# Merge of a hybrid decoder layer: the samples' columns of the attention's values are prepared in one step, apart from the prompt's

## The chip, the cores and the metric

The kernel runs on one core of one Trainium2 chip. The metric is the device time of one execution in microseconds (us), the median of the runs shown; lower is better.

## What is computed

One step of a decoder layer with two parallel branches: stick-breaking attention and a state space layer. It handles a prompt of 1024 tokens and 8 samples of one token each, whose columns are kept side by side (1024 + 8 = 1032 columns, channels on the partitions). The part that matters here is the end, where the branches meet; the reference, cut to it:

```python
def _finish(x, gate, o_att, g_att, y_ssm, m_att, m_ssm, w_att_out, w_out, ln_g, ln_b):
    y_att = (o_att.reshape(bsz, s, D_ATT) * jax.nn.silu(g_att)) @ w_att_out
    merged = jax.nn.sigmoid(m_att) * y_att + jax.nn.sigmoid(m_ssm) * y_ssm
    return _layer_norm(DEEPNORM_ALPHA * x + gate * (merged @ w_out), ln_g, ln_b)
```

`o_att` are the attention's values, `silu(g_att)` their gate, `y_ssm` the output of the state space layer's own last product (`y @ w_ssm_out`). `gate` comes from a small product of the conditioning vector with `w_cond`.

## The kernel before

All large products are made in float32 accuracy out of three products of halves: an operand is split into `hi`, its value rounded by a cast on ScalarE (ACT), and `lo`, the rest, by a subtraction on VectorE (DVE). `gemm` (L124 to L144) makes one slab of 128 output channels: 8 input blocks, 3 thirds of 344 columns and 3 pairs of halves, 72 matmuls in all, into three PSUM tiles `pj`; its weights `whi` and `wlo` are split while the slab before runs.

The order of TensorE (PE) is that in which the program is written. `Stream` holds the queue of slabs; `weave` (L211 to L222) deals a list of other steps evenly between the matmuls: in front of each step it runs a share of what is left of the slabs in the queue. Its argument `until` is the amount of slab work at which it stops. The order of the other engines and of the DMA queues is set by a scheduler that plans with estimated times; it too is fixed when the program is built. An instruction that waits holds up all that stands behind it on its engine.

The merge, at the end of the program (from L1614 on), runs four groups of eight slabs and then the output product:

- `glu` (L1224), the gated unit of the state space layer.
- `ssm_out` (L1251), its output product. Slab f is evacuated on DVE with three products (L1261, tile `m`, which came from `d_mm`) and written to `d_pa` (L1262).
- `att_out` (L1291), the attention's output product over `act_a`, the eight split blocks of the attention's values; it adds what lies in `d_pa`.
- `finish` (L1359), the output product and the normalization.

Three kinds of small work are dealt into `ssm_out`. First the rest of `LateValues` (L845): the samples' attention reads the last pages of its value cache here, by gathers into `l_t`, products (L884) and sums (L885) on DVE, a last addition (L888), and then writes the samples' values to `d_o` in memory (L889). They are woven in until 5 slabs are left (L1635). Then, by L1636, two lists of eight steps each, dealt alternately over what is left:

- `gate_steps` (L1321): a gate part is four matmuls (L343, tile `gp`) on a block of `w_cond` that was loaded (L327) and split (L334 on ACT, L335 on DVE). The halves `wchi` and `wclo` have one buffer each, so the split for the next part starts behind the matmuls of this one.
- `open_a` (L1268): step f prepares one block of the attention's values. Three loads of 512 KB, the values in two halves and their gate (`x` at L1198, `olo` at L1278, `sga` at L1279), an addition (L1280) and a product (L1281) on DVE make the prompt's 1024 columns. For the samples' 8 columns, a row block `orow` of 8 × 128 is loaded from `d_o` (L1283), transposed on PE (L1285, tile `otp`) and multiplied by its gate `sgs` on DVE (L1286). Then all 1032 columns are split in one go: a cast on ACT (L234) and a subtraction on DVE (L235).

Buffers couple these. The tag `wc` has four: the gathered `l_t`, the blocks of `w_cond`, `olo`, `sga` and later blocks of `w_out` take them in turn. The tag `x` has two. The PSUM tiles `gp` and `otp` share two buffers of one tag.

Of the kernel before, what the change touches and what calls it, by code (L numbers as in the profile page):

```python
# [9 lines left out]
F32 = mybir.dt.float32  # L10
F32R = mybir.dt.float32r
I32 = mybir.dt.int32
AF = mybir.ActivationFunctionType
ALU = mybir.AluOpType
# [3 lines left out]
NP, NS, NT = 1024, 8, 1032  # L18
NC3, CW = 3, 344
KT = 8  # L20
# [8 lines left out]
MM = 146.0  # L29
# [4 lines left out]
HURRY = 400  # L34
# [6 lines left out]
NLATE = 26  # L41
GS = "v"
LATE = 5.0
AHEAD = 2
DRAIN = 1.6
TWO_PI = 6.283185307179586
# [35 lines left out]
def blk(i, w=128):  # L82
    return slice(w * i, w * i + w)
# [141 lines left out]
def weaved(a, b):  # L225

    n = [((i + 0.5) / len(x), j, s) for j, x in enumerate((a, b)) for i, s in enumerate(x)]
    return [s for _, _, s in sorted(n, key=lambda e: e[:2])]


def split_act(k, pool, src):
    hi = pool.tile([128, NT], F32R, tag="hi", bufs=KT, name="ahi")
    lo = pool.tile([128, NT], F32R, tag="lo", bufs=KT, name="alo")
    k.nc.scalar.copy(hi, src)  # L234
    k.nc.vector.tensor_tensor(lo, src, hi.bitcast(F32), ALU.subtract)  # L235
    return hi, lo
# [301 lines left out]
class Attention:  # L538
# [130 lines left out]
    def turn(self, p, h, m, j):  # L669

        k, nc, pool = self.k, self.k.nc, self.pool
        PE, ACT, DVE = nc.tensor, nc.scalar, nc.vector
        w = [self.w[p, h, 2 * m + e][0] for e in range(2)]
        tp = self.ps.tile([128, 4, 128], F32, tag="wt", name="tp")
        if j < m:
            hi, lo = (pool.tile([128, 4, 128], F32R, tag=n, bufs=LAG + 1, name=n) for n in ("wthi", "wtlo"))
        else:
            hi, lo = self.diag
        order = (0, 1) if j < m else (1, 0)
        for a in order:  # L680
            for e in range(2):
                if j < m or (a, e) != (1, 0):
                    PE.transpose(tp[:, 2 * order[a] + e], w[e][:, blk(2 * j + a)], k.ident)  # L683
        with k.tc.high_priority(HURRY):
            s = slice(0 if j < m else 1, 4)
            ACT.copy(hi[:, s], tp[:, s])  # L686
            DVE.tensor_tensor(lo[:, s], tp[:, s], hi[:, s].bitcast(F32), ALU.subtract)  # L687
        return hi, lo
# [39 lines left out]
    def steps(self, pairs):  # L728

        units = [(p, h, ms) for p in pairs for h in range(2) for ms in ((3, 0), (2, 1))]  # L730
        out = {p: [] for p in pairs}
        for u, (p, h, ms) in enumerate(units):
            s = self.score_steps(units[u + 1]) if u + 1 < len(units) else []
            t = [(860, (lambda key=(p, h, m): self.ready_at[key]) if j == ORDER[m][0] else None,
                  lambda t=(p, h, m, j): self.turn_step(t)) for m in ms for j in ORDER[m]]
            if not s:
                t += [(430, None, lambda: self.turn_step(None))] * LAG
            seq = []
            for n in (2, 2, 1, 1):
                seq += s[:n] + t[:1]  # L740
                s, t = s[n:], t[1:]
            out[p] += seq + t
        return self.score_steps(units[0]), out
# [101 lines left out]
class LateValues:  # L845
# [25 lines left out]
    def step(self, n):  # L871

        k, nc = self.k, self.k.nc
        if n < 8 * self.pages:
            self.load(n // 8, n % 8)
        n -= AHEAD
        if n < 0:
# [13 lines left out]
    def steps(self):  # L891
        return [(0, None, lambda n=n: self.step(n)) for n in range(8 * self.pages + AHEAD)]

# [296 lines left out]
class Merge:  # L1190
# [77 lines left out]
    def open_a(self):  # L1268

        k, nc = self.k, self.k.nc  # L1270
        self.a_guard = self.pool("seta", "right")
        pa = self.a_guard.__enter__()
        self.act_a = []

        def one(f):
            t = self.load(k.d_a[f, 0], "x", NP)
            o, s = (self.ld.tile([128, NP], F32, tag="wc", bufs=4, name=n) for n in ("olo", "sga"))
            nc.sync.dma_start(o, k.d_a[f, 1])  # L1278
            nc.sync.dma_start(s, k.d_sa[f])  # L1279
            nc.vector.tensor_tensor(t[:, 0:NP], t[:, 0:NP], o, ALU.add)  # L1280
            nc.vector.tensor_tensor(t[:, 0:NP], t[:, 0:NP], s, ALU.mult)  # L1281
            ob = self.ld.tile([NS, 128], F32, tag="orow", bufs=2, name="orow")
            nc.sync.dma_start(ob, k.d_o[:, blk(f)])  # L1283
            tp = k.psg.tile([128, 512], F32, tag="g", name="otp")
            nc.tensor.transpose(tp[:, 0:NS], ob, k.ident[0:NS, 0:NS])  # L1285
            nc.vector.tensor_tensor(t[:, NP:NT], tp[:, 0:NS], k.sgs[:, f], ALU.mult)  # L1286
            self.act_a.append(split_act(k, pa, t))

        return [(110, None, lambda f=f: one(f)) for f in range(KT)]

    def att_out(self):  # L1291
        k, nc = self.k, self.k.nc
# [160 lines left out]
def stickbreak_s5_kernel(ctx: ExitStack, tc: tile.TileContext, io, out):  # L1453
    nc = tc.nc
    k = Ctx()
# [55 lines left out]
    S = k.stream = Stream(k)  # L1511
# [108 lines left out]
    mg = Merge(k, io, out)  # L1620
# [12 lines left out]
    mg.open_gate()  # L1633
    mg.ssm_out()
    S.weave(late[NLATE:], LATE * KT * 9 * MM)  # L1635
    S.weave(weaved(mg.gate_steps(), mg.open_a()))  # L1636
    mg.s_guard.__exit__(None, None, None)
    mg.att_out()
    mg.open_out()
# [60 lines left out]
def build(nc, arrays):  # L1700
    from concourse import mybir as _mybir
    io = {n: nc.dram_tensor("in_" + n, v.shape, _mybir.dt.from_np(v.dtype), kind="ExternalInput").ap()
          for n, v in arrays.items()}
    out = {n: nc.dram_tensor("out_" + n, s, F32, kind="ExternalOutput").ap() for n, s in _OUTS}
    with tile.TileContext(nc, schedule_with_timeline_sim=True) as tc:
        stickbreak_s5_kernel(tc, io, out)
# [12 lines left out]
```

## Time and profile before

| | |
|---|---|
| median of 3 runs | 1613.56 us (1612.72 to 1615.05) |
| the profiled execution, its own time | 1617.42 us |
| span in its profile, first to last instruction | 1615.7 us |
| PE busy | 1489.5 us, 92% of the span |
| DVE, POOL (GpSimd), ACT busy | 1218.9, 911.0, 736.5 us |
| mean granted clock of PE | 0.969 |
| PE busy in 1300 to 1350, 1350 to 1414, 1414 to 1504 us | 32.75 of 50, 60.05 of 64, 90.00 of 90 us |

A row of a timeline gives start and duration in us, the engine, the line of the kernel, the operation, what it writes and reads by the program's names, the shape, and in brackets how long the engine stood idle ahead of it and what ended that. `SPq` and `ACTq` are the issues of DMAs by those engines. Matmuls overlap: the rows last 0.32 us where one starts every 0.16, so the distance of starts is what counts. A row of the waits gives the total, the number of times and the longest. The chain of waits goes back from the last instruction, at each step to what released it.

### The profile page before, as it was taken

What the parts mean: (1) busy time and instruction counts of PE and PEld (TensorE: products, weight loads), DVE (VectorE), ACT (ScalarE), POOL (GpSimd) and SP (SyncE); (2) the same over time, 40 slices, a digit from 0 to 9 for tenths busy, and PEclk for the clock granted to TensorE, in tenths of its full rate; (3) what the DMA queues carried; (4) which work ended last, traced back from release to release, by engine and by line L of the source; (5) the groups of instructions that cost most, each with busy time, mean ns of one, the idle gap of its engine ahead of it and who ended that gap; (6) DMA issues with size and microseconds to landing.
All of it is one profiled execution on the core that took longest, in us unless ns stands there. A gap on an engine that the chain in (4) does not pass through costs nothing.

```text
span 1615.7 us, 25524 instructions
## 1 busy us (share of the span) xinstructions
PE 1489.5 (92%) x9321; PEld 1410.2 (87%) x9321; DVE 1218.9 (75%) x1717; ACT 736.5 (46%) x1360; POOL 911.0 (56%) x744
## 2 busy tenths in 40 slices
PE   8899999999999999999989978889979786999997
PEld 4789999999999998999888978889779685899885
DVE  5558888888888888743899978787489975744566
ACT  3557777777776776643433333333432212311200
POOL 1738787878777877766566555552176541132164
PEclk9899999999999999999999989999989997999999
DMA  9323433334343434348789887875546677954322
GB/s 356 111 82 89 104 100 97 99 97 113 87 113 93 115 88 111 101 123 288 246 266 287 265 265 249 285 235 132 164 158 222 213 249 261 348 180 140 118 79 91
DMA packets 176731, 275.47 MB, mean 170 GB/s; under 512 B 46395, under 2 KB 119867, under 8 KB 176477
## 3 DMA queue, kind: packets, MB, share of 16 engines
q1 hardware_dynamic: 150555, 180.40, 36.6%
q0 software_dynamic: 23456, 84.95, 16.4%
q10 hardware_dynamic: 2594, 8.49, 2.0%
q8 instruction: 73, 1.20, 0.3%
q14 instruction: 53, 0.43, 0.1%
HBM read 196.77 MB, written 66.24 MB: 163 GB/s over the span
## 4 chain that ended last, share of the span: by engine, by line
PE 49%; DVE 26%; DMA 9%; issue 5%; ACT 3%; POOL 2%; SPq 1%; DVEq 0%; ACTq 0%; POOLq 0%
PE pj L141 32%; PE f L1397 6%; DVE s_sc L828 4%; PE o L700 3%; PE z L654 3%; PE tp L683 3%; DVE ke L665 3%; DVE l_t L884 2%; DMA s_t<-in_cache_k,s_idx 2%; DVE be L666 2%; DVE vs L636 2%; DMA l_t<-in_cache_v,l_idx 2%; DVE l_acc L885 2%; DVE wlo L109 1%; DVE xs L1037 1%
## 5 line engine op out<-in xcount | busy, mean ns | idle before, releaser
L141 PE MATMUL pj<-ahi,whi 128*128 128x344 f32 x2112 | 695.4, 331 | 36.8 <-ACT u L970 17.5
L141 PE MATMUL pj<-alo,whi 128*128 128x344 f32 x2112 | 686.1, 326 | 7.9 <-DVE alo L1220 4.1
L141 PE MATMUL pj<-ahi,wlo 128*128 128x344 f32 x2112 | 581.6, 328 | 6.0 <-POOL wlo L109 6.0
L141 PEld LDWEIGHTS pj<-ahi,whi 128*128 128x128 f32 x2112 | 405.6, 192 | 45.9 <-ACT u L970 18.3
L141 PEld LDWEIGHTS pj<-alo,whi 128*128 128x128 f32 x2112 | 405.6, 192 | 11.9 <-DVE alo L235 4.9
L141 PEld LDWEIGHTS pj<-ahi,wlo 128*128 128x128 f32 x2112 | 382.6, 192 | 8.0 <-POOL wlo L109 6.5
L665 DVE TENSOR_TENSOR_SCAN ke<-ke,eye 128x896 f32<-128x896 f32 (+7 forms) x128 | 217.7, 1701 | 92.4 <-ACT ke L655 92.2
L109 POOL TENSOR_TENSOR wlo<-w,whi 128x1024 fp32r<-128x1024 f32 x53 | 141.6, 2672 | 207.7 <-ACT whi L108 178.8
L108 ACT CAST whi<-w 128x1024 fp32r<-128x1024 f32 x90 | 94.9, 1055 | 137.3 <-PE pj L141 100.1
L655 ACT ACTIVATE ke<-z,nhb 128x448 f32<-128x448 f32 (+2 forms) x192 | 111.8, 582 | 81.1 <-PE z L654 79.2
L666 DVE TENSOR_TENSOR be<-be,ke 128x896 f32<-128x896 f32 (+7 forms) x128 | 128.0, 1000 | 13.0 <-ACT wthi L686 0.5
L828 DVE SCALAR_TENSOR_TENSOR s_sc<-s_t,s_q,s_sc 128x512 f32<-128x512 f32 x126 | 114.0, 905 | 18.0 <-DMA s_t<-in_cache_k,s_idx 12.0
L656 ACT ACTIVATE be<-z,hb 128x448 f32<-128x448 f32 (+2 forms) x192 | 110.6, 576 | 0.0
L807 POOL DMA_INDIRECT s_t<-in_cache_k,s_idx x64 | 70.6, 1103 | 50.8 <-DVE s_sc L828 15.5
L683 PE MATMUL tp<-ident,be 128*128 128x128 f32 x576 | 88.9, 272 | 0.0
L493 POOL TENSOR_TENSOR pt<-tab 128x256 f32<-128x256 f32 x64 | 79.5, 1241 | 3.1
L492 POOL TENSOR_TENSOR pr<-tab 128x256 f32<-128x256 f32 x32 | 25.9, 811 | 89.4 <-DMA tab<-d_tab 78.7
L1520 ACT ACTIVATE gate<-pj 128x344 f32<-128x344 f32 x72 | 32.7, 458 | 95.4 <-PE pj L141 86.5
L109 DVE TENSOR_TENSOR wlo<-w,whi 128x1024 fp32r<-128x1024 f32 x37 | 62.5, 1689 | 15.4 <-ACT whi L108 15.3
L686 ACT CAST wthi<-tp 128x512 fp32r<-128x512 f32 x96 | 56.7, 590 | 32.3 <-PE tp L683 29.9
L654 PE MATMUL z<-kl,qs 128*128 128x448 f32 (+2 forms) x192 | 66.0, 344 | 4.0 <-DMA kl<-kl 4.0
L687 DVE TENSOR_TENSOR wtlo<-tp,wthi 128x512 fp32r<-128x512 f32 x96 | 65.3, 680 | 5.7 <-ACT wthi L686 5.7
(314 smaller groups left out, 2758.5 us busy)
## 6 DMA issues: line engine op xcount, KB each, us to landing
w<-in_w_in SPq DMA_DIRECT2D x38, 512.0 KB
w<-in_w_in POOLq DMA_DIRECT2D x26, 512.0 KB, 5.6
wc<-in_w_cond SPq DMA_DIRECT2D x24, 512.0 KB
d_a<-ox SPq DMA_DIRECT2D x128, 64.0 KB
gst<-d_gg SPq DMA_DIRECT2D x8, 576.0 KB
x<-in_xr SPq DMA_DIRECT2D x9, 512.0 KB
xt<-in_xt SPq DMA_DIRECT2D x8, 516.0 KB
d_sg<-gate SPq DMA_DIRECT2D x8, 516.0 KB
```

What stands on the lines that cost most here:

```text
L108: nc.scalar.copy(whi, w32)
L109: self.eng.tensor_tensor(wlo, w32, whi.bitcast(F32), ALU.subtract)
L141: PE.matmul(ps[c], w[:, blk(t)], x[:, cs(c)], start=(t == 0 and i == 0), stop=(t == KT - 1 and i == 2))
L493: POOL.tensor_tensor(t1, c, d, ALU.mult)
L654: nc.tensor.matmul(z[:, 0:wide], st["q", h][:, blk(i)], x[:, s:s + wide], start=j == 0, stop=j == 1)
L655: nc.scalar.activation(ke[:, s:s + cw], z[:, 0:cw], AF.Sigmoid, bias=k.nhb[:, hd:hd + 1], scale=-0.125)
L656: nc.scalar.activation(be[:, s:s + cw], z[:, 0:cw], AF.Sigmoid, bias=k.hb[:, hd:hd + 1], scale=0.125)
L665: nc.vector.tensor_tensor_scan(rev, rev, self.eye[:, NP - n:][:, ::-1], 0.0, ALU.mult, ALU.add)
L666: nc.vector.tensor_tensor(be, be, ke[:, 1:n + 1], ALU.mult)
L683: PE.transpose(tp[:, 2 * order[a] + e], w[e][:, blk(2 * j + a)], k.ident)
L828: DVE.scalar_tensor_tensor(sc, t, q[:, d - d0:d - d0 + 1], sc, op0=ALU.mult, op1=ALU.add)
L1397: PE.matmul(pp[c], a[:, token(i)], w[:, blk(c, 512)], start=(t == 0 and a is ah and w is wh), stop=(t == KT - 1 and a is al))
```

## The change

`open_a` keeps only the prompt's columns: loads, addition, product and a split of 1024 columns. A new step, `samples_a`, prepares the samples' 8 columns of all eight blocks together: one load of the whole of `d_o` (8 × 1024, into a `wc` buffer), eight transposes into one PSUM tile, one product of 128 × 64, and eight splits of 128 × 8 into the last columns of the same `hi` and `lo` tiles. The weave of gate parts and blocks ends when 1.6 slabs of `ssm_out` are left instead of none (`ROWS`), and the new step is woven into these 1.6 slabs, with a raised priority for the scheduler.

```diff
+ROWS = 1.6
...
-        def one(f):
-            t = self.load(k.d_a[f, 0], "x", NP)
+        def prompt(f):
+            t = self.load(k.d_a[f, 0], "x", NP)[:, 0:NP]
             o, s = (self.ld.tile([128, NP], F32, tag="wc", bufs=4, name=n) for n in ("olo", "sga"))
             nc.sync.dma_start(o, k.d_a[f, 1])
             nc.sync.dma_start(s, k.d_sa[f])
-            nc.vector.tensor_tensor(t[:, 0:NP], t[:, 0:NP], o, ALU.add)
-            nc.vector.tensor_tensor(t[:, 0:NP], t[:, 0:NP], s, ALU.mult)
-            ob = self.ld.tile([NS, 128], F32, tag="orow", bufs=2, name="orow")
-            nc.sync.dma_start(ob, k.d_o[:, blk(f)])
-            tp = k.psg.tile([128, 512], F32, tag="g", name="otp")
-            nc.tensor.transpose(tp[:, 0:NS], ob, k.ident[0:NS, 0:NS])
-            nc.vector.tensor_tensor(t[:, NP:NT], tp[:, 0:NS], k.sgs[:, f], ALU.mult)
-            self.act_a.append(split_act(k, pa, t))
-
-        return [(110, None, lambda f=f: one(f)) for f in range(KT)]
+            nc.vector.tensor_tensor(t, t, o, ALU.add)
+            nc.vector.tensor_tensor(t, t, s, ALU.mult)
+            hi = pa.tile([128, NT], F32R, tag="hi", bufs=KT, name="ahi")
+            lo = pa.tile([128, NT], F32R, tag="lo", bufs=KT, name="alo")
+            nc.scalar.copy(hi[:, 0:NP], t)
+            nc.vector.tensor_tensor(lo[:, 0:NP], t, hi[:, 0:NP].bitcast(F32), ALU.subtract)
+            self.act_a.append((hi, lo))
+
+        return [(0, None, lambda f=f: prompt(f)) for f in range(KT)]
+
+    def samples_a(self):
+
+        k, nc = self.k, self.k.nc
+        ob = self.ld.tile([NS, NP], F32, tag="wc", bufs=4, name="orow")
+        nc.sync.dma_start(ob, k.d_o)
+        tp = k.psg.tile([128, 512], F32, tag="g", name="otp")[:, 0:64].rearrange("p (f s) -> p f s", f=KT)
+        t = self.ld.tile([128, KT, NS], F32, tag="orow", bufs=1, name="os")
+
+        def turn():
+            for f in range(KT):
+                nc.tensor.transpose(tp[:, f], ob[:, blk(f)], k.ident[0:NS, 0:NS])
+            with k.tc.high_priority(HURRY):
+                nc.vector.tensor_tensor(t, tp, k.sgs, ALU.mult)
+                for f in range(KT):
+                    hi, lo = (x[:, NP:NT] for x in self.act_a[f])
+                    nc.scalar.copy(hi, t[:, f])
+                    nc.vector.tensor_tensor(lo, t[:, f], hi.bitcast(F32), ALU.subtract)
+
+        return [(900, None, turn)]
...
-    S.weave(weaved(mg.gate_steps(), mg.open_a()))
+    S.weave(weaved(mg.gate_steps(), mg.open_a()), ROWS * KT * 9 * MM)
+    S.weave(mg.samples_a())
```

The change also moves instructions. Numbers behind names tell buffers of one tile apart; lines below L1272 have other numbers in the changed kernel (L1261 is L1262 there, L1281 is L1282, L1285 is L1301).

PE in slab 3 of `ssm_out` before, at the first of the eight transposes (`pj_14244` to `pj_14246` are the thirds of slab 3):

```order
L141 MATMUL pj_14244<-ahi_13552,wlo_14140 128x344
L141 MATMUL pj_14245<-ahi_13552,wlo_14140 128x344
L1285 MATMUL otp_14312<-ident_68,orow_14310 128x8
L141 MATMUL pj_14246<-ahi_13552,wlo_14140 128x344
L141 MATMUL pj_14244<-ahi_13670,whi_14139 128x344
```

PE now, where all eight stand, between slab 6 (`pj_14680`) and slab 7 (`pj_14808`):

```order
L142 MATMUL pj_14680<-ahi_13902,whi_14534 128x344
L142 MATMUL pj_14680<-alo_13903,whi_14534 128x344
L142 MATMUL pj_14680<-ahi_13902,wlo_14535 128x344
L1301 MATMUL otp_14732<-ident_68,orow_14730 128x8 x8
L142 MATMUL pj_14808<-ahi_13076,whi_14674 128x344
```

The eight transposes moved from eight places in slabs 3 to 7 to one.

DVE before, at the end of the late values (`l_acc`), which the first samples' product follows (`x_14302` is block 0, `wclo_14277` belongs to the second gate part):

```order
L885 TENSOR_REDUCE l_acc_12719<-l_t_14095 128x8
L885 TENSOR_REDUCE l_acc_12719<-l_t_14130 128x8
L335 TENSOR_TENSOR wclo_14277<-wc_13919,wchi_14276 128x1024
L888 TENSOR_TENSOR l_acc_12719<-l_acc_12719 128x64
L1280 TENSOR_TENSOR x_14302<-x_14302,olo_14304 128x1024
L1281 TENSOR_TENSOR x_14302<-x_14302,sga_14305 128x1024
L1280 TENSOR_TENSOR x_14363<-x_14363,olo_14365 128x1024
L1281 TENSOR_TENSOR x_14363<-x_14363,sga_14366 128x1024
L1286 TENSOR_TENSOR x_14302<-otp_14312,sgs_75 128x8
L235 TENSOR_TENSOR alo_14316<-x_14302,ahi_14315 128x1032
```

DVE now at the same place (block 0 is `x_14288`, the second gate part's half `wclo_14270`, the third's `wclo_14322`):

```order
L886 TENSOR_REDUCE l_acc_12719<-l_t_14095 128x8
L336 TENSOR_TENSOR wclo_14270<-wc_13919,wchi_14269 128x1024
L886 TENSOR_REDUCE l_acc_12719<-l_t_14130 128x8
L889 TENSOR_TENSOR l_acc_12719<-l_acc_12719 128x64
L336 TENSOR_TENSOR wclo_14322<-wc_14267,wchi_14321 128x1024
L1281 TENSOR_TENSOR x_14288<-x_14288,olo_14290 128x1024
L1262 TENSOR_TENSOR m_14236<-pj_14244,m_14236 128x344
L1262 TENSOR_TENSOR m_14236<-pj_14245,m_14236 128x344
L1282 TENSOR_TENSOR x_14288<-x_14288,sga_14291 128x1024
```

The second gate part's subtraction stands one reduction earlier, and the third's ahead of the first block.

DVE now at the end of slab 5 of `ssm_out`, whose thirds are `pj_14538` to `pj_14540` (`wclo_14563` and `wclo_14613` belong to the last two gate parts):

```order
L336 TENSOR_TENSOR wclo_14563<-wc_14494,wchi_14562 128x1024
L1281 TENSOR_TENSOR x_14518<-x_14518,olo_14520 128x1024
L1262 TENSOR_TENSOR m_14530<-pj_14538,m_14530 128x344
L1282 TENSOR_TENSOR x_14518<-x_14518,sga_14521 128x1024
L861 COPY l_p_14659<-m_14530 128x1
L1262 TENSOR_TENSOR m_14530<-pj_14539,m_14530 128x344
L1262 TENSOR_TENSOR m_14530<-pj_14540,m_14530 128x344
L1286 TENSOR_TENSOR alo_14527<-x_14518,ahi_14526 128x1024
L336 TENSOR_TENSOR wclo_14613<-wc_14560,wchi_14612 128x1024
```

DVE before around the evacuation of slab 5 (`pj_14535` to `pj_14537`; `wclo_14651` and `wclo_14735` belong to the last two gate parts):

```order
L1261 TENSOR_TENSOR m_14527<-pj_14535,m_14527 128x344
L1261 TENSOR_TENSOR m_14527<-pj_14536,m_14527 128x344
L860 COPY l_p_14642<-m_14527 128x1
L1261 TENSOR_TENSOR m_14527<-pj_14537,m_14527 128x344
L335 TENSOR_TENSOR wclo_14651<-wc_14567,wchi_14650 128x1024
L1280 TENSOR_TENSOR x_14689<-x_14689,olo_14691 128x1024
L1281 TENSOR_TENSOR x_14689<-x_14689,sga_14692 128x1024
L1286 TENSOR_TENSOR x_14689<-otp_14699,sgs_75 128x8
L235 TENSOR_TENSOR alo_14703<-x_14689,ahi_14702 128x1032
```

Before, the seventh gate part's subtraction followed the evacuation of slab 5 and the eighth's came in slab 7; now the eighth's stands behind the evacuation of slab 5.

## The prediction

> **What bounds the kernel now.** I read the page first, then the waits of TensorE (PE) over the merge, from 1130 us to the end, then the timelines of PE, VectorE (DVE), ScalarE (ACT) and the SP queue around the longest of them, last the DMA by window. The eight products of the state space output are called slabs 0 to 7, the eight gate parts g0 to g7 (each four matmuls gp), the eight blocks of the attention's values b0 to b7.
>
> The page: PE is the busiest engine, so what counts is where it stands still.
>
> ```profile
> span 1615.7 us, 25524 instructions
> PE 1489.5 (92%) x9321; PEld 1410.2 (87%) x9321; DVE 1218.9 (75%) x1717; ACT 736.5 (46%) x1360; POOL 911.0 (56%) x744
> ```
>
> The waits of PE over the merge (total us, times, longest): the one that this change touches is the longest, and two smaller ones lie in the same stage.
>
> ```profile
> PE otp L1285 <- DMA orow<-d_o: 17.2, 1, 17.2
> PE gp L343 <- DVE x L1286: 2.6, 1, 2.6
> PE gp L343 <- DVE wclo L335: 1.4, 2, 0.8
> ```
>
> The timeline of PE (start, us, what, idle before and what ended it), and then the chain of waits to the end of the stage:
>
> ```profile
> 1325.38 0.40 PE L343 MATMUL gp<-wchi,csplit 128*128 128x512 f32 x1
> ...
> 1347.17 0.27 PE L1285 MATMUL otp<-ident,orow 8*128 8x8 f32 x1 [17.25 <-DMA orow<-d_o]
> ...
> 1376.12 0.47 PE L343 MATMUL gp<-wchi,csplit 128*128 128x512 f32 x1 [2.57 <-DVE x L1286]
> 1377.15 0.50 PE L343 MATMUL gp<-wclo,csplit 128*128 128x512 f32 x1 [0.57 <-DVE wclo L335]
> ```
> ```profile
> 1378.21 5.22 PE pj L141 x24
> ...
> 1387.54 0.93 PE gp L343 x4
> ...
> 1392.24 0.15 PE otp L1285
> ...
> 1410.07 94.46 PE pj L141 x600
> ```
>
> A matmul starts every 94.46/600 = 0.157 us, a slab of 72 takes 11.34, a gate part 0.93, a transpose 0.15. The 24 matmuls behind the waits of 2.57 and 0.57 us took 5.22 instead of 24 × 0.157 = 3.77: a wait of some 3 us costs 1.45, say 1.5 us more in slower matmuls, and I count the same behind any longer one. The 600 matmuls from 1410.07 are 24 of slab 7 and all 576 of the attention output, which therefore begins at 1410.07 + 24 × 0.157 = 1413.85. From there on both kernels do the same, so the difference is when that point is reached.
>
> Why the first transpose waits, on DVE, ACT and SP:
>
> ```profile
> 1333.60 2.33 DVE L885 TENSOR_REDUCE l_acc<-l_t 128x8 f32<-128x1024 f32 x2
> 1335.85 1.21 DVE L335 TENSOR_TENSOR wclo<-wc,wchi 128x1024 fp32r<-128x1024 f32 x1
> 1336.98 0.21 DVE L888 TENSOR_TENSOR l_acc<-l_acc 128x64 f32<-128x64 f32 x1
> 1339.52 1.23 DVE L1280 TENSOR_TENSOR x<-x,olo 128x1024 f32<-128x1024 f32 x1 [2.33 <-DMA olo<-d_a]
> ...
> 1349.47 1.23 DVE L235 TENSOR_TENSOR alo<-x,ahi 128x1032 fp32r<-128x1032 f32 x1 [1.12 <-ACT ahi L234]
> 1351.63 0.52 DVE L1261 TENSOR_TENSOR m<-pj,m 128x344 f32<-128x344 f32 x1 [0.92 <-PE pj L141]
> ...
> 1356.82 2.57 DVE L335 TENSOR_TENSOR wclo<-wc,wchi 128x1024 fp32r<-128x1024 f32 x1
> ```
> ```profile
> 1330.76 1.04 ACT L334 CAST wchi<-wc 128x1024 fp32r<-128x1024 f32 x1 [7.70 <-DVE m L1261]
> 1337.23 0.33 ACTq L889 DMA_DIRECT2D d_o<-l_acc  x1
> ```
> ```profile
> 1331.43 0.38 SPq L327 DMA_DIRECT2D wc<-in_w_cond  x1
> ...
> 1342.80 0.63 SPq L1283 DMA_DIRECT2D orow<-d_o  x2
> ```
>
> The samples' values are complete only at 1337.19 (L888), go out to d_o at 1337.23 and are read back from 1342.80. PE, whose order is fixed by the program, may do nothing else meanwhile.
>
> **The change part by part.** *The eight transposes leave the weave.* The 17.25 us wait goes, and with it the 2.57: there gp needed a PSUM buffer that a transpose's tile still held. What is late next is g1, which now comes 30 matmuls behind g0. I follow PE in the changed kernel's order. g0 stands 15 matmuls into slab 3, 7 fewer than before: 1325.38 - 7 × 0.157 = 1324.3. g1 is reached at 1324.3 + 0.93 + 30 × 0.157 = 1329.9, but its wclo follows the first of the last two reductions: half of 2.33 behind 1333.60 is 1334.7, plus 1.21 is 1335.9. A wait of 6.0 us takes the place of the 17.25, with the same 1.5 us of slow matmuls, 0.3 of it in g1, which ends at 1335.9 + 0.93 + 0.3 = 1337.1.
>
> *The gate parts come closer together.* The 16 steps share 3.4 slabs instead of 5, so gate parts are 27 to 33 matmuls apart, some 6 us instead of 9. g2 is reached at 1337.1 + 27 × 0.157 + 1.2 = 1342.5; its load (issued 1331.43) and its wchi and wclo (1.04 + 1.21 behind g1) are there at 1339.6. Slab 4 starts at 1343.5 and with g3 and g4 ends at 1343.5 + 11.34 + 1.86 = 1356.7. From there DVE's fixed order is late three times, each time because a wclo stands behind work that has a wait of its own (a matmul ends 0.2 behind its slot, and a cast is handed on in 0.1):
> - g5, 15 matmuls into slab 5, is reached at 1359.1. Its wclo stands behind the last evacuation of slab 4 (0.52) and a product with sga (1.23 like the addition): 1356.7 + 0.2 + 0.52 + 1.23 + 1.21 = 1359.8. Wait 0.7.
> - g6 is reached at 1359.8 + 0.93 + 27 × 0.157 = 1365.0. Between the two wclo stand a subtraction, an addition, a product, ACT's cast and another subtraction: 4 × 1.23 + 1.04 + 0.2 + 1.21 = 7.4, so 1367.2. Wait 2.2, which I count without slow matmuls (with them 1.5 more).
> - g7 ends slab 5, reached at 1367.2 + 0.93 + 4.24 = 1372.4. Its wclo stands behind the evacuation of that slab's last third, which cannot begin earlier, and a subtraction: 0.2 + 0.52 + 1.23 + 1.21 = 3.2, so 1375.6. Wait 3.2, and 1.5 behind it.
>
> Behind g7's start come 0.93, slab 6 (11.34), the eight transposes (8 × 0.15 = 1.2) and slab 7 (11.34): 24.8. The attention output begins at 1375.6 + 1.5 + 24.8 = 1401.9, which is 11.95 us earlier.
>
> The Trainium skill ("TensorE: Matmul & The Clock Gate", "What's actually happening") says that the clock falls to half after an idle window of about 3.4 us. By that rule the 3.2 us at g7 would leave the clock alone in most cases, and the gain would be 1.5 us more; the trace has the slow 24 matmuls behind 2.57 + 0.57 us, so the 1.5 stays.
>
> *The transfers are asked for faster.* DMA by window (us; PE, PEld, DVE, ACT, POOL busy; clock, DMA share, GB/s), and the size of a load:
>
> ```profile
> 1330.00:1378.00 48.00, 26.87 (x144) 24.56 (x145) 31.11 (x36) 10.94 (x12) 5.92 (x2) 0.82 0.76 247
> 1378.00:1414.00 36.00, 36.00 (x210) 34.52 (x209) 27.62 (x35) 11.81 (x13) 4.80 (x2) 0.95 0.99 373
> 1324.00:1330.00 6.00, 5.93 (x36) 5.47 (x34) 5.27 (x5) 0.00 (x0) 4.01 (x3) 1.00 0.64 210
> ```
> ```profile
> wc<-in_w_cond SPq DMA_DIRECT2D x8, 512.0 KB
> ```
>
> In SP's new order 17 loads of 0.524 MB stand from g4's wc to g7's, both included, and two writes of d_pa fall among them: 10.0 MB. The first goes out when b0's product with sga frees its buffer, behind slab 3's first evacuations, at about 1343.5. At 373 GB/s the last lands at 1370.3, and its cast and subtraction (2.3) fit ahead of 1375.6. At 247 it lands at 1384.0, and g7, at 1386.3, is 10.7 us later. The 247 came at a share of 0.76, so the engines were not full: 247/0.76 = 325 at full use. I take that, since the new order asks for more at once: 30.8 us, landing 1374.3, g7 at 1376.6, 1.0 us later than above.
>
> *One slow DVE operation.* At 1356.82 a subtraction of this form took 2.57 us instead of 1.21. DVE now paces g5 to g7, so I count one of them: 1.3 us, between 0 and 4.
>
> *The samples' own step.* Eight orow loads of 4 KB become one of 32 KB, behind b7's loads in SP's order; for eight products there are one product, eight small casts and eight small subtractions. Rows of these shapes by group (count, busy, mean ns):
>
> ```profile
> L1219 ACT CAST ahi<-ygs 128x8 fp32r<-128x8 f32 x8 | 1.9, 237 | 0.3 <-DVE ygs L1085 0.3
> L1220 DVE TENSOR_TENSOR alo<-ygs,ahi 128x8 fp32r<-128x8 f32 x8 | 3.6, 450 | 0.0
> L1286 DVE TENSOR_TENSOR x<-otp,sgs 128x8 f32<-128x8 f32 x8 | 1.2, 156 | 0.7 <-PE otp L1285 0.7
> ```
>
> The casts and subtractions are at most 1.9 + 3.6 = 5.5 us, under slab 7's 11.34; uncovered they would cost those 5.5. The split of b7 now stands behind the transposes on DVE and ACT, and has slab 7 and most of the attention output's first product (b7 is its last block) as cover. orow needs the buffer that b6's addition frees, about 6 us behind g7, and then 4.4 (issued 1342.80, used 1347.17): 1376.6 + 10.4 = 1387.0, against 1376.6 + 0.93 + 11.34 + 1.5 = 1390.4 for PE. Covered by 3 us.
>
> The sum: 11.95 - 1.0 - 1.3 = 9.65 us less. The profiled execution took 1617.42 us, 1.7 more than its span, and would take 1607.8; it lies 3.86 above the median of 1613.56, so against that I forecast 1603.9.
>
> **The rivals.**
> - *Transfers become the bound, slower.* The stage asks for 10 MB in some 30 us where the same kinds of load ran at 247 GB/s. At 240 and less (landing 41.7 us behind 1343.5) nothing is gained. At the 210 of 1324 to 1330 the last wc lands at 1391.1, g7 starts at 1393.4, 17.8 us behind 1375.6, and the sum is 17.8 - 11.95 = 5.9 us slower: 1619.4. For it: a buffer must still come free for every issue. Against it: 373 GB/s right behind, with the same loads. Chance 0.07.
> - *Transfers hold it about level.* At 240 to 265 GB/s the landing is at 1381 to 1385 and the gain 0 to 4 us: about 1611.5. Chance 0.09.
> - *orow comes late.* If it is held by b7's loads for more than the 3 us of cover, PE waits at the transposes with all of slab 7 unplayed. At 4 us beyond the cover the gain is 5.6: 1607.9. Chance 0.12.
> - *DVE is not late at g5 and g6.* Then 0.7 + 2.2 of waiting go, and neither the slow operation nor the transfers are met: 11.95 + 2.9 = 14.85 less, 1598.7. Chance 0.06.
>
> That the change doesn't do what it says is excluded by the order of PE: the transposes stand behind slab 6.
>
> **How the numbers follow.** The forecast, a gain of 7 to 13 us, has 0.66. The range is 1598 to 1611.5: its ends are the fuller gain and the level case, and the slower case is left out. What can be told from no change is 0.2%, 3.2 us. Faster by more: 0.66 + 0.12 + 0.06 = 0.84; within: 0.09; slower: 0.07.
>
> **What would show it.** In the profile after: no wait on orow of more than a few us; a wait of about 6 us of gp on wclo near 1336; waits of gp on wclo of 1 to 3 us towards the end of slab 5; the attention output beginning near 1404; over 300 GB/s between 1345 and 1375. The forecast is wrong if PE stands still for more than 15 us between g0 and the attention output, or if a wait behind that is longer than before.

## The result and the profile after

The changed kernel takes 1606.21 us (median of 5 runs, 1604.56 to 1608.66) against 1615.05 us (1612.72 to 1617.32) for the kernel before, measured beside it: ratio 0.9949, 95% interval 0.9933 to 0.9966, or 8.2 us less (5.5 to 10.8). Measured once more, beside three of the experiments, the ratio was 0.9949 (0.9931 to 0.9966). The profiled execution took 1608.66 us, its span 1607.0 against 1615.7 before.

The page of after, top. PE works as long as before (1490.9 against 1489.5 us); what has gone is standing still.

```profile
span 1607.0 us, 25517 instructions
...
PE 1490.9 (93%) x9321; PEld 1410.2 (88%) x9321; DVE 1212.6 (75%) x1718; ACT 736.8 (46%) x1368; POOL 906.4 (56%) x744
```

The waits of PE over the merge after (total us, times, longest). The transposes no longer appear at all, and the gate parts, which had waited 2.6 + 1.4 us, now wait 12.8.

```profile
PE gp L344 <- DVE wclo L336: 7.3, 3, 3.6
PE gp L344 <- ACT wchi L335: 5.5, 3, 2.9
```

The same waits in the timeline of PE after, two rows each for g1, g5 and g7, the only gate parts that wait:

```profile
1330.40 0.49 PE L344 MATMUL gp<-wchi,csplit 128*128 128x512 f32 x1 [1.43 <-ACT wchi L335]
1334.53 0.79 PE L344 MATMUL gp<-wclo,csplit 128*128 128x512 f32 x1 [3.64 <-DVE wclo L336]
...
1359.10 0.51 PE L344 MATMUL gp<-wchi,csplit 128*128 128x512 f32 x1 [1.17 <-ACT wchi L335]
1361.27 0.50 PE L344 MATMUL gp<-wclo,csplit 128*128 128x512 f32 x1 [1.67 <-DVE wclo L336]
...
1376.59 0.79 PE L344 MATMUL gp<-wchi,csplit 128*128 128x512 f32 x1 [2.92 <-ACT wchi L335]
1379.35 0.79 PE L344 MATMUL gp<-wclo,csplit 128*128 128x512 f32 x1 [1.97 <-DVE wclo L336]
```

The four waits of the kernel before between g0 and the attention output (17.25, 0.82, 2.57, 0.57) add up to 21.2 us, the six here to 12.8. The difference, 8.4 us, accounts for the gain.

The chain of waits after, from g7 to the output product (start, duration, what), and the output product's row of the kernel before:

```profile
1380.99 12.15 PE pj L142 x72
1393.14 0.59 PE otp L1301 x8
1393.72 102.06 PE pj L142 x648
1495.79 100.63 PE f L1417 x432
```
```profile
1504.53 100.63 PE f L1397 x432
```

Slab 7 is the first 72 of the 648 matmuls, so the attention output begins at 1393.72 + 72 × 0.1575 = 1405.06 (1413.85 before). That is 8.8 us earlier; 0.5 of it came in ahead of the merge's weave, as slab 0 shows, whose only wait ends at these places, after and before:

```profile
1292.07 0.65 PE L142 MATMUL pj<-ahi,whi 128*128 128x344 f32 x1 [8.51 <-ACT ahi L235]
```
```profile
1292.54 0.65 PE L141 MATMUL pj<-ahi,whi 128*128 128x344 f32 x1 [8.71 <-ACT ahi L234]
```

Across profiles this place moves by up to 10 us, for reasons ahead of everything that is edited here. So I compare profiles by the **stage**: from that row to the start of the output product. It is 1504.53 - 1292.54 = 211.99 us before and 1495.79 - 1292.07 = 203.72 after, 8.3 shorter, in line with the ratio.

### The profile page after: what moved, and what is told of

It reads as the page before. It is cut to its first block, busy times and chain, and to the rows that moved or that the text cites. A ratio compares the mean times of both kernels' runs of the same rounds, so it can differ in the third digit from the quotient of the medians.

```text
span 1607.0 us, 25517 instructions
## 1 busy us (share of the span) xinstructions
PE 1490.9 (93%) x9321; PEld 1410.2 (88%) x9321; DVE 1212.6 (75%) x1718; ACT 736.8 (46%) x1368; POOL 906.4 (56%) x744
## 4 chain that ended last, share of the span: by engine, by line
PE 48%; DVE 26%; DMA 9%; issue 6%; POOL 2%; ACT 2%; SPq 2%; DVEq 0%; POOLq 0%; ACTq 0%
PE pj L142 31%; PE f L1417 6%; PE o L701 4%; PE z L655 3%; DVE ke L666 3%; PE tp L684 3%; DVE s_sc L829 3%; DVE l_t L885 2%; DVE vs L637 2%; DVE be L667 2%; DVE l_acc L886 2%; DMA l_t<-in_cache_v,l_idx 2%; DVE s_t L824 1%; DMA s_t<-in_cache_v,s_idx 1%; DVE m L1245 1%
## 5 line engine op out<-in xcount | busy, mean ns | idle before, releaser
L666 DVE TENSOR_TENSOR_SCAN ke<-ke,eye 128x896 f32<-128x896 f32 (+7 forms) x128 | 223.4, 1745 | 92.5 <-ACT ke L656 92.1
L667 DVE TENSOR_TENSOR be<-be,ke 128x896 f32<-128x896 f32 (+7 forms) x128 | 119.8, 936 | 13.0 <-ACT wthi L687 0.5
L494 POOL TENSOR_TENSOR pt<-tab 128x256 f32<-128x256 f32 x64 | 74.5, 1164 | 3.1
```

The lines of the kernel that those rows point to most:

```text
L494: POOL.tensor_tensor(t1, c, d, ALU.mult)
L666: nc.vector.tensor_tensor_scan(rev, rev, self.eye[:, NP - n:][:, ::-1], 0.0, ALU.mult, ALU.add)
L667: nc.vector.tensor_tensor(be, be, ke[:, 1:n + 1], ALU.mult)
```

## The experiments

Theory, from the profile after: the wait for orow was worth all of its 17 us, and squeezing the gate parts and blocks into 3.4 slabs gives half of it back. Rivals: the change's own step for the samples costs the rest; or 8 us is all that the wait was worth, because something else would have been late anyway. The table has all runs; the gain in us is one minus the ratio, times the median of before beside it (1614.9 to 1616.5). A plus is faster, and in the last columns are the stage in the profile and PE's waits in it from g0 on, each from one profile.

| kernel | ratio (95%) | gain us | stage us | waits of PE, us |
|---|---|---|---|---|
| before | | | 211.99 | 21.2 |
| after | 0.9949 (0.9933 to 0.9966) | +8.2 | 203.72 | 12.8 |
| after once more | 0.9949 (0.9931 to 0.9966) | +8.2 | 205.64 | 13.7 |
| rows that are ready | 0.9891 (0.9861 to 0.992) | +17.6 | 195.57 | 5.3 |
| squeezing alone | 0.9992 (0.9969 to 1.0016) | +1.3 | 210.67 | 19.3 |
| spread as before | 0.9896 (0.9878 to 0.9913) | +16.8 | 196.23 | 7.1 |
| to 0.8 slabs | 0.9919 (0.9888 to 0.995) | +13.1 | 199.66 | 9.7 |
| without olo | 0.9873 (0.9832 to 0.9913) | +20.5 | 192.12 | 5.3 |
| rows ahead of b6 | 0.9881 (0.986 to 0.9903) | +19.2 | 193.28 | 6.1 |
| the same once more | 0.9878 (0.9856 to 0.99) | +19.7 | 191.80 | 3.5 |
| late values spread further | 0.9901 (0.988 to 0.9922) | +16.0 | 196.73 | 8.9 |
| gate parts back by one block | 0.9899 (0.9877 to 0.9921) | +16.3 | 197.72 | 10.3 |
| gate parts back by two | 0.9993 (0.9979 to 1.0007) | +1.1 | 208.17 | 17.0 |
| wlo on VectorE | 0.9945 (0.992 to 0.9969) | +8.9 | 202.36 | 11.4 |

**Rows that are ready.** The kernel before, whose eight small loads read memory that was written long ago (the samples' values are left out).

```diff
-            nc.sync.dma_start(ob, k.d_o[:, blk(f)])
+            nc.sync.dma_start(ob, k.d_q[:, blk(f)])
```

> The kernel before with one edit: the eight row blocks orow are read from the samples' queries, which lie in memory long before, instead of from the attention's values (so the samples' attention values are left out). The transposes stay where they are, nothing is compressed. Theory, pacing (the gain of the change is the wait for orow, partly given back because the steps come closer together than DVE, ACT and the transfers can follow): the 17.2 us wait goes, a wait of about 4 us at the second gate part and its slow matmuls take its place, and later waits stay below 3 us in sum; 11 to 14 us faster than before, so 2 to 5 us faster than the changed kernel. Rival, transfers (the loads of the stage set its length whatever the order): no more than the changed kernel's 8.8 us, with a DMA share near 1.0 from 1345 to 1375.

The whole wait came back, 17.6 us (16.4 by the stage), more than either number. PE's waits in that kernel, over the merge: only the gate parts' 5.3 us remain of the stage.

```profile
PE gp L343 <- DVE wclo L335: 5.3, 2, 4.0
```

So nothing else was late by 8 us behind orow as long as the weave stays wide, and the second rival falls.

**Squeezing alone.** The kernel before, with its gate parts and blocks (transposes among them) ending 1.6 slabs early.

```diff
-    S.weave(weaved(mg.gate_steps(), mg.open_a()))
+    S.weave(weaved(mg.gate_steps(), mg.open_a()), ROWS * KT * 9 * MM)
+    S.drain()
```

> The kernel before with only the other half of the change: the weave of gate parts and blocks ends when 1.6 slabs are left, the transposes and 1032-column splits stay in each block's step. Pacing: the wait for orow stays, 17 to 19 us, and the closer steps add 3 to 6 us of waits at later gate parts; 1 to 6 us slower than before. If the closer steps cost nothing, the time is that of before, within 2 us.

No change, so the expectation missed. The waits of PE show why:

```profile
PE otp L1286 <- DMA orow<-d_o: 16.3, 1, 16.3
...
PE gp L344 <- DVE wclo L336: 3.0, 2, 2.2
```

PE still stands for 16.3 us at the first transpose, and the gate parts behind it wait for only 3.0, where the same spacing without that wait costs 12.8: while PE stands, loads, casts and subtractions run ahead. The price of squeezing is hidden under the wait that the change removes; the two edits don't add up.

**Spread as before.** The changed kernel with `ROWS = 0.0`: the samples' one step stays, the squeezing goes.

> The changed kernel with the gate parts and blocks spread as before the change: g0 to g7 stand at 4.69, 4.08, 3.68, 3.06, 2.67, 2.0, 1.33 and 0.67 slabs ahead of the end of the output (in the changed kernel at 4.79 to 2.0), and the samples' one step comes behind slab 7, with nothing of the output left to cover it. Theory (squeezing eight blocks into 2.8 slabs makes the waits at g5 and g7, and the late reductions the one at g1; the place of the samples' step needs cover behind b7's loads): the waits at g5 to g7 go (4.9 and 2.8 us to below 1 each), and the transposes wait for orow and the first product behind them for eight conversions, 5 to 12 us: 2 to 9 us faster than before the change, so as the changed kernel or slower. Rival (the compression was never needed, one step for the samples is all): as the kernel with a spacing to 0.8 slabs or better, 13 to 17 us faster than before.

16.8 us faster than before, twice the change's gain, and where the rival had put it: the squeezing was not needed. The waits at g5 to g7 went as the theory has it, but its price for the uncovered step was wrong. PE waits for 0.5 us at the transposes and 2.5 us at the attention output's first columns that need the samples:

```profile
PE gp L344 <- DVE wclo L336: 4.1, 2, 2.6
PE pj L142 <- DVE alo L1307: 2.5, 1, 2.5
...
PE otp L1301 <- DMA orow<-d_o: 0.5, 1, 0.5
```

The 2.5 us are hardly the conversions themselves. DVE's eight small subtractions, and POOL (GpSimd) beside them:

```profile
1394.63 2.85 DVE L1307 TENSOR_TENSOR alo<-os,ahi 128x8 fp32r<-128x8 f32 x8
```
```profile
1393.96 2.96 POOL L110 TENSOR_TENSOR wlo<-w,whi 128x1024 fp32r<-128x1024 f32 x1 [11.65 <-ACT whi L109]
```

The first of the eight takes 2.31 us, the others 0.16; it ends with POOL (1396.94 and 1396.92), as if held by it; the last experiment takes up such operations. So the samples' step doesn't eat the gain: with nothing left to cover it, it costs 3 us, some 2 of them for this first operation, while the rest runs beside the attention output's first matmuls. The 1.6 slabs kept for it cost about 8.

**To 0.8 slabs.** The changed kernel with `ROWS = 0.8`.

> The changed kernel with ROWS = 0.8 instead of 1.6: the 16 steps get 4.2 slabs instead of 3.4, the samples' step comes 0.4 slabs ahead of the end. Pacing: the waits at the gate parts fall from 12.8 us to 6 to 8 (the 5 us at the second one stay), 11 to 14 us faster than before. Transfers: about the same 9 us as with 1.6, since the same bytes have to come. Rival, samples: the small splits no longer fit ahead of the attention output; a wait of 2 us and more of PE on them at its start, and 6 to 9 us faster than before.

13.1 us faster, as the pacing theory has it. Most of the gate parts' waits are gone (5.5 us are left), but now the transposes wait. PE, and then the last two issues on SP ahead of it:

```profile
1386.74 0.63 PE L1301 MATMUL otp<-ident,orow 8*128 8x8 f32 x8 [4.15 <-DMA orow<-d_o]
```
```profile
1381.12 0.32 SPq L1199 DMA_DIRECT2D x<-d_a  x1
1382.25 0.29 SPq L1295 DMA_DIRECT2D orow<-d_o  x1
```

The load of orow stands behind b7's three on SP's queue and takes 4.5 us from issue to use (4.4 in the kernel before). Its values were sent to d_o at 1328.58 in this profile. What held it was its place in the queue, and there a `wc` buffer: SP waits 0.7 us for the addition (L1281) that frees one at 1382.22.

**Without olo.** The changed kernel without the eight loads of olo, the gate tile added in its place: 4.2 of 12.6 MB of the blocks' loads, and the low halves of the values, are left out.

> The changed kernel with the second half of the values (olo) not loaded; the addition takes the gate tile in its place, so DVE does as many operations (the low half of the values is left out). 4 MB less to load in the stage. Transfers: the waits of the fifth gate part and later vanish (from 7.7 us to below 1.5), the wait of 5 us at the second stays; 14 to 17 us faster than before. Pacing by the fixed order of DVE and ACT: with a DMA share clearly below 0.9 from 1345 to 1375 waits of 3 us and more remain there; 9 to 12 us faster.

20.5 us faster, no gate part waits behind g1, and the transfers are no longer full between 1345 and 1375 (columns as in the prediction; this kernel, then after):

```profile
1345.00:1375.00 30.00, 30.00 (x185) 29.29 (x185) 26.19 (x28) 9.93 (x10) 5.40 (x2) 1.00 0.88 319
```
```profile
1345.00:1375.00 30.00, 25.83 (x144) 24.28 (x142) 24.21 (x26) 9.22 (x10) 2.65 (x2) 0.94 1.01 376
```

So the loads of olo are behind the late waits. It is not proof that their bytes are: without olo a block takes one `wc` buffer, not two, so that later loads can be issued sooner, and the scheduler also put g7's subtraction ahead of slab 5's evacuation on DVE. The next kernel and the one spread as before speak against bytes alone.

**Rows ahead of b6.** `ROWS = 0.8`, and the load of orow issued before the last two blocks ask for theirs (`rows_a` holds the two lines that load it, taken out of `samples_a`).

```diff
-    S.weave(weaved(mg.gate_steps(), mg.open_a()), ROWS * KT * 9 * MM)
+    steps = weaved(mg.gate_steps(), mg.open_a())
+    S.weave(steps[:-3] + [(0, None, mg.rows_a)] + steps[-3:], ROWS * KT * 9 * MM)
```

> The changed kernel with the blocks spread until 0.8 slabs are left, and the load of the samples' rows issued ahead of b6's loads, not behind b7's. Theory (with that spacing the 4.15 us at the transposes were a wait for a load that was queued behind b7's, while its rows had been in memory since 1330): the wait at the transposes goes, nothing else changes, 3 to 5 us faster than that spacing with the load behind b7: 15 to 18 us faster than before the change. Rival (the loads ahead of it in the queue are what is short, so that b6 and b7 come later by as much): a wait of 2 to 4 us at g7 or at the first product of the attention output in its place, 12 to 13 us faster than before.

> The kernel with the rows ahead of b6 once more, beside the two others on their chip. Both theories: 17 to 20 us faster than before the change, one wait of 5 to 7 us at g1, none behind it.

19.2 and 19.7 us faster than before: against the changed kernel, measured beside the first of them at 1605.88 us, 1596.50. These are the lowest times of a kernel that does the whole computation; the one spread as before (1597.67 beside 1596.50) can't be told from it. The gain is a little above what either theory had for the first. From g0 to the attention output PE waits once, at g1, for 6.1 us (3.5 in the second profile, where 5 to 7 were expected):

```profile
PE gp L344 <- DVE wclo L336: 6.1, 1, 6.1
```

The transfers are as full as in the changed kernel, and so they are in the one spread as before (both from 1345 to 1375, in this order), and PE waits for nothing in that window:

```profile
1345.00:1375.00 30.00, 30.00 (x184) 29.17 (x183) 27.25 (x27) 10.67 (x11) 5.61 (x2) 1.00 1.00 382
```
```profile
1345.00:1375.00 30.00, 30.00 (x185) 29.30 (x184) 25.61 (x26) 10.29 (x12) 5.36 (x2) 1.00 1.02 401
```

This fits a reading in which what counts is whether the gate parts ask for a load before the queue can have brought it; no run tests that by itself.

> The changed kernel itself once more, beside the three others on their chip. Both theories: 7 to 10 us faster than before the change; the stage from the end of slab 0's first wait to the start of the last product is 203.7 us long in its first profile and is expected within 1 us of that, whatever its span.

Gain and waits as before; the stage was 205.64 us, 1.9 longer than in the first profile, outside the 1 us that I had allowed. Differences of stages under 2 us should not be read.

**The wait at g1.** Two ways to give g1 more room, on top of the rows ahead of b6. First `LATE = 4.5`:

> As the kernel with the rows ahead of b6, and the late values are given half a slab more (spread until 4.5 slabs are left, not 5), so that g1 stands at 3.79 slabs ahead of the end and not at 4.29, and the gate parts lie in 3.0 slabs and not in 3.5. Theory (g1 waits 3.6 us because its low weights stand behind the last reductions on VectorE): the wait at g1 goes and a little of the later ones comes back: 1 to 4 us faster than with the rows ahead of b6 alone, 17 to 20 us faster than before the change. Rival (the reductions move with the gate parts, or the parts crowd in the last slabs): the wait stays or moves to g5 to g7, no faster or 1 to 3 us slower than with the rows ahead of b6 alone.

g1 came half a slab later and waited as long (0.9 + 5.1 us). The time is where the rival had it, but its reason fails for g1: the last reductions ended at 1333.59, and g1's subtraction stood on DVE behind b0's addition, which waited for its load and was then slow:

```profile
1337.36 2.46 DVE L1281 TENSOR_TENSOR x<-x,olo 128x1024 f32<-128x1024 f32 x1 [3.08 <-DMA olo<-d_a]
...
1339.81 1.21 DVE L336 TENSOR_TENSOR wclo<-wc,wchi 128x1024 fp32r<-128x1024 f32 x1
```

Then the gate parts put back against the blocks, by two and by one:

```diff
-    steps = weaved(mg.gate_steps(), mg.open_a())
-    S.weave(steps[:-3] + [(0, None, mg.rows_a)] + steps[-3:], ROWS * KT * 9 * MM)
+    g, b = mg.gate_steps(), mg.open_a()
+    steps = weaved(g[:6], b[2:])
+    S.weave(b[:2] + steps[:-3] + [(0, None, mg.rows_a)] + steps[-3:] + g[6:], ROWS * KT * 9 * MM)
```

> The kernel with the rows ahead of b6 (which waits 6.05 us once, at g1, for its low weights), with the gate parts put back by two blocks: b0 and b1 come ahead of g0, and g6 and g7 behind b7, so that g1 stands at 4.0 slabs ahead of the end of the output, not 4.29, with the late values where they were. Theory (the wait is for the late reductions that stand ahead of those weights on VectorE, and 0.29 slab is 3.3 us of matmuls, so the rest of the wait is 2 to 3 us): 3 to 5 us faster than with the rows ahead of b6 alone, 21 to 24 us faster than before the change. Rival (VectorE is full there, b0 and b1 now stand ahead of g1's weights with three operations each, 1.2 us apiece): g1 comes 3 to 7 us later on VectorE, the wait stays at 5 to 8 us, no faster than with the rows ahead of b6 alone.

> As the one before with one block, not two, ahead of g0: g1 at 4.06 slabs ahead of the end. Theory: a wait of 2.5 to 3.5 us at g1, 2 to 4 us faster than with the rows ahead of b6 alone. Rival: 4 to 7 us at g1, no faster than with the rows ahead of b6 alone.

Both missed, and the rival is right in the place: a block's operations now stand ahead of g1's weights. By one block g1 waits 4.2 us and g2 3.0. By two blocks nearly the whole gain is lost. DVE there, ahead of g1's matmul, which starts at 1344.11:

```profile
1339.55 1.22 DVE L1282 TENSOR_TENSOR x<-x,sga 128x1024 f32<-128x1024 f32 x1 [1.97 <-DMA sga<-d_sa]
1340.69 3.36 DVE L336 TENSOR_TENSOR wclo<-wc,wchi 128x1024 fp32r<-128x1024 f32 x1
```

g1's subtraction now stands behind a block's product that waits for its load, so VectorE isn't full there, as the rival had it, but idle for 1.97 us; and the subtraction itself takes 3.36 us where 1.21 is usual. g7, behind b7, waits 4.4 us for its cast. How the wait at g1 could be removed stays open. A part of it that no run here takes out by itself is the last gather of the late values: with the rows ahead of b6 alone DVE stands idle for it, ahead of g1's subtraction (2.00 us in the second profile, where PE waits 3.5 and not 6.1):

```profile
1331.00 1.23 DVE L885 TENSOR_TENSOR l_t<-l_t,l_sc 128x1024 f32<-128x1024 f32 x1 [3.05 <-DMA l_t<-in_cache_v,l_idx]
```

**wlo on VectorE.** The operations of 1.21 us that take over 2 are no accident. In the changed kernel, POOL subtracting wlo, and then DVE:

```profile
1356.63 2.37 POOL L110 TENSOR_TENSOR wlo<-w,whi 128x1024 fp32r<-128x1024 f32 x1 [11.70 <-ACT whi L109]
1374.72 2.36 POOL L110 TENSOR_TENSOR wlo<-w,whi 128x1024 fp32r<-128x1024 f32 x1 [15.71 <-ACT whi L109]
```
```profile
1357.32 2.77 DVE L1282 TENSOR_TENSOR x<-x,sga 128x1024 f32<-128x1024 f32 x1
...
1375.62 2.53 DVE L1286 TENSOR_TENSOR alo<-x,ahi 128x1024 fp32r<-128x1024 f32 x1 [1.24 <-ACT ahi L1285]
```

Each long one ends 1.07 to 1.09 us behind the end of the wlo beside it (1360.09 behind 1359.00, 1378.15 behind 1377.08), as if it had started only then. The kernel before has it too: each of POOL's four wlo from 1350 to 1414 has such an operation beside it (2.57, 2.92, 2.58 and 2.21 us). The edit takes POOL out from slab 4 on:

```diff
     S.weave(late[NLATE:], LATE * KT * 9 * MM)
+    k.w.eng = nc.vector
```

> The changed kernel with the weights' low halves subtracted on VectorE, not on GpSimd, from slab 4 of the output on. Theory (a subtraction of two tensors on VectorE that begins while GpSimd makes a wlo is held until GpSimd is done: in the changed kernel the long ones of 2.22, 2.77, 2.53 and 3.29 us, where others of their form take 1.21, end 1.1 us behind the end of the wlo beside each): no operation of 1024 columns on VectorE takes over 1.4 us between 1340 and 1412. In time this is worth little, since each slab adds 1.21 us to VectorE and takes away 1.0 to 2.1: within 3 us of the changed kernel, 5 to 12 us faster than before the change. Rival (the long ones come from the transfers, which are full at 376 GB/s, and from chance): two to four operations of over 2 us remain in that window; VectorE has 1.21 us more for each slab, so g5 to g7 wait 1 to 4 us longer, 4 to 8 us faster than before.

The groups of DVE between 1330 and 1412 us (count, busy, mean ns), without POOL, then after:

```profile
L1282 DVE TENSOR_TENSOR x<-x,sga 128x1024 f32<-128x1024 f32 x8 | 9.8, 1223 | 0.2
...
L1286 DVE TENSOR_TENSOR alo<-x,ahi 128x1024 fp32r<-128x1024 f32 x8 | 9.7, 1218 | 2.2 <-ACT ahi L1285 2.2
L336 DVE TENSOR_TENSOR wclo<-wc,wchi 128x1024 fp32r<-128x1024 f32 x7 | 8.5, 1221 | 0.6 <-ACT wchi L335 0.6
...
L110 DVE TENSOR_TENSOR wlo<-w,whi 128x1024 fp32r<-128x1024 f32 x6 | 7.3, 1220 | 0.4 <-ACT whi L109 0.4
```
```profile
L1282 DVE TENSOR_TENSOR x<-x,sga 128x1024 f32<-128x1024 f32 x8 | 13.4, 1674 | 0.3 <-DMA sga<-d_sa 0.2
L1286 DVE TENSOR_TENSOR alo<-x,ahi 128x1024 fp32r<-128x1024 f32 x8 | 11.0, 1380 | 3.5 <-ACT ahi L1285 3.5
...
L336 DVE TENSOR_TENSOR wclo<-wc,wchi 128x1024 fp32r<-128x1024 f32 x7 | 9.5, 1361 | 2.7 <-ACT wchi L335 2.7
```

All means fall to 1.22 us, and no operation of 1024 columns takes over 1.4 us between 1340 and 1412: the long operations were held by POOL. The time stays that of the changed kernel, and PE's waits nearly so (11.4 us; 12.8 and 13.7 there): DVE pays 7.3 us for six wlo (one of them at the window's edge) and gets back 3.6 + 1.3 + 1.0 = 5.9. The Trainium skill ("SBUF — State Buffer", "SBUF: two separate sides") says that VectorE, when it reads two inputs from SBUF, and GpSimd, when it reads SBUF, share a pair of ports which the first to start holds for its whole instruction; the rows agree. The evacuations `m<-pj,m`, whose one input lies in PSUM, are not held: two of them take 0.93 us from 1356.47 on, with POOL's wlo running from 1356.63.

## Why the prediction was right, point by point

I forecast 9.65 us less; the ratio gives 8.2, the stage 8.3. Most terms are right in size and cause; the shares of g5, g6 and g7 are not, and that their sum came out is in part luck.

- *The transposes leave the weave.* Right: the waits of 17.25 and 2.57 us are gone. The run with rows that are ready shows that the first was worth about its whole length.
- *g1.* Right in place and cause, 5.07 us instead of 6.0. From its last wait to g2 it took 1341.30 - 1334.53 = 6.8 us where 3 × 0.23 + 27 × 0.157 = 4.9 were due at full speed, so the slow matmuls cost 1.8 (1.5 assumed). The prediction took the place of the reductions as given; part of it is POOL's doing, by this row of DVE after:

```profile
1324.74 3.23 DVE L885 TENSOR_TENSOR l_t<-l_t,l_sc 128x1024 f32<-128x1024 f32 x1 [1.59 <-DMA l_t<-in_cache_v,l_idx]
```

  It ends 1.09 us behind a wlo of POOL, takes 2.0 us more than others of its form, and from there DVE has work without a gap until g1's subtraction ends at 1334.48. With wlo on VectorE it takes 1.23, and g1 waits 4.5 us although one wlo more stands ahead of it on DVE. The wait at g1 is there in every run but the one in which the transposes still wait ahead of it: 3.5 to 7.7 us, at g1 or shared by two gate parts.
- *g5, g6, g7.* The sum was nearly right, 0.7 + 2.2 + 3.2 and 2.3 for transfers and a slow operation, 8.4 in all, against 2.84 + 0 + 4.89 = 7.7. The shares were not, and their errors (+2.1, -2.2 and +1.7, with the 2.3 not spent apart) cancelled. (Between g5 and g6 stand 30 matmuls, not the 27 counted, so the forecast wait at g6 should have been 1.7; the time of g7 doesn't hang on it.) g5 waited longer: its load landed late (ACT idle for 1.45 us on it), and behind it stood the long product of 2.77 us. g6 then came so late itself that all was ready. At g7 I missed ACT's queue. Its rows after:

```profile
1373.60 1.04 ACT L109 CAST whi<-w 128x1024 fp32r<-128x1024 f32 x1 [6.50 <-PE pj L142]
...
1374.55 1.04 ACT L1285 CAST ahi<-x 128x1024 fp32r<-128x1024 f32 x1
1375.49 1.04 ACT L335 CAST wchi<-wc 128x1024 fp32r<-128x1024 f32 x1
```

  The cast for g7 stands behind that of slab 7's weights, which may only begin when slab 5 lets go of the buffer, and behind b4's: PE waits 2.92 us for it, and 1.97 more for DVE, where I had only DVE.
- *Transfers.* I took 325 GB/s, they ran at 376 between 1345 and 1375, at a share of 1.01, so neither rival with transfers at 265 and less came true; the 1.0 us that I charged to g7's load was spent at g5's and in ACT's queue instead.
- *One slow operation, 1.3 us.* Two stood ahead of g5 and g7, 2.77 and 2.53 us where 1.21 is usual, and not by chance: of POOL's five wlo between 1340 and 1412 four held one. So the term was right to stand in the sum, but for a reason that the prediction did not have.
- *orow covered.* Right: issued at 1385.33, 7.8 us ahead of the transposes (3 us of cover were forecast beyond the 4.4 of a load), and no wait. The rival that it comes late was sound as a mechanism: with 0.8 slabs it decides, for 4.15 us.
- *Behind g7.* 24.8 + 1.5 us were forecast from g7's start to the attention output; from 1379.35 it took 25.7.

What the prediction did not see is that the change gives half of its gain away. It costed the closer gate parts against PE's places, wait by wait, and got their size, and it had a price for the samples' step without cover, 5.5 us (3 measured); it never set that price against what the 1.6 slabs of cover cost, about 8.

## What to carry to other kernels

When a long wait in an in-order engine goes, the steps behind it lose the time in which their loads and casts ran ahead: cost them again at the new distances, and squeeze them only as far as the covered step needs. Read at the issuing queue how long a late load has been possible; here issuing 32 KB two blocks earlier took away a wait of 4.15 us, with half of the squeezing. A step costs what it leaves uncovered, so measure it once with no cover before paying for some.

## What the runs showed of the hardware

- A DVE operation of two SBUF tensors of 1024 columns that POOL's subtraction of a 128x1024 tile holds up ends 1.07 to 1.10 us after POOL does, in every profile here (in the changed kernel between 1340 and 1412 such operations take 2.22 to 3.29 us instead of 1.22); a 128x8 one ended with POOL (2.31 us instead of 0.16). With POOL's subtractions moved to DVE none there is long.
- Behind a wait of PE the matmuls can be slow for a few us: the granted clock (1.00 is full speed) is 0.51 from 1334.60 to 1338.40 in the changed kernel, behind 3.64 us. The first matmul (128x512) behind a single wait takes 0.47 to 0.51 us up to 2.64, 0.79 to 0.80 from 3.09 on, and either around 2.9 (0.79 and 0.62 behind 2.92, 0.50 behind 2.95). Both 2.92 and 3.09 are shorter than the idle window of about 3.4 us that the prediction quotes from the Trainium skill ("TensorE: Matmul & The Clock Gate", "What's actually happening"); here the measurement decides. The length of one wait doesn't settle it: 1.73 to 2.14 us shortly behind another wait were followed by 0.79 to 0.80 too, and behind 2.64 the first took 0.50 but the clock over the next 2.9 us was 0.67.
- DMA ran at 374 to 401 GB/s at a share of 1.00 to 1.02 from 1345 to 1375 us in the changed kernel and in four others. With the rows ahead of b6 (382 GB/s) and spread as before (401) PE was busy for all 30.00 us of it: full transfers are not by themselves a wait.
